# Full-height filter and value products, small loads on a second queue, and four reorderings, in a two-block sequence kernel

## The chip, the cores and the metric

The kernel runs on one core of a Trainium2 chip. The metric is the device time of one launch in microseconds (us): 2917.35 is the median of three runs (2915.61 to 2918.12). The engines that matter are TensorE (PE; its weight loads are listed apart as PEld), VectorE (DVE), ScalarE (ACT), GpSimd (POOL) and SyncE (SP), which issues nearly all transfers.

## The reference

The input is x (512 tokens of 1024 numbers) and a context ctx (256 tokens). Two blocks follow one another, all in float32.

- First block: `mod = silu(c) @ w_ada + b_ada` gives shifts, scales and gates ("vectors"). `rms_norm(x)` and `rms_norm(ctx)` are modulated with them and projected with `w_in` into keys, values, queries and gates of retention and mLSTM scans, whose outputs are merged; then a SwiGLU layer and a final `rms_norm`.
- Second block: four layers; before each, `cond @ w_mod[layer] + b_mod[layer]` gives its vectors.
  - Layers 0 and 3: latent attention, softmax over 768 keys.
  - Layer 1: windowed attention with a sink, `p = softmax(concat(scores + [sink]))`, `out = p @ v`.
  - Layer 2: Hyena, two long convolutions with filters `h = (sin(...) @ f_w3) * exp(-t * deltas)`.
  - Each layer ends with `x = x + gate * rmsnorm(y @ w_out, g_post)`; the last x is the output.

## The kernel before

Activations lie transposed in SBUF: eight tiles (k) of 128 features by 512 tokens (256 for ctx). A product in float32 accuracy is three float32r products on a high and a low part (`mac`, L441 to L443: hi*hi, hi*lo, lo*hi). `split` (L397, L398) makes the parts, the high one on ACT and the low one on DVE. Weights come through four `raw` buffers of 512 KB, issued on SP (`wload`, L403).

The kernel is written as generators that `weave` runs side by side in given proportions. A scheduler then orders each engine's instructions; every engine executes its own in order, and so does SP's queue.

- Start (`first_block`): SP issues small vectors and the filters' small tables, then x, ctx and the weights `w_ada` (L504 multiplies them, two transfers a step, four steps a vector). x and ctx are transposed (L490), squared and summed (L231, L235), normed (`apply`: L570 and L576 on DVE, L575 on ACT, for eight tiles of x and then eight of ctx). The first pair's keys are one complete product for each of two heads; rope (L781 to L783) follows, then the keys of ctx.
- Filters (`filter_unit`, L1873, L1874), woven into the SwiGLU layer: `ps = x @ w + x[0:64] @ l`, where x holds 64 high rows over 64 low rows, w the high weights twice, l the low weights in 64 rows. There are 48 such pairs.
- Windowed attention: `stageA` makes scores and softmax of a block of 128 queries for four heads one after the other, `stageB` transposes the probabilities and multiplies with the values, stored as 64 high columns beside 64 low ones: `v` (128 columns) by p.hi (L1739), `v.hi` (64 columns) by p.lo (L1738, L1741). `softmax` closes each head by itself: a sink exponential (L1387), a sum (L1388), a reciprocal (L1389).
- Hyena: four channel groups c; group c's convolutions (i = 0 for x, 1 for ctx) are woven with the projections of c+1. After the third round come ctx's convolution of the last group and nine steps of x's, woven with the next layer's vectors (`bg`, eight steps) and the layer end's first loads (`end`).
- Layer end: groups of 256 tokens: product, copy and squares, root of the mean square (PE, DVE, POOL), its spread over partitions (L1373), scaling and adding x (L1308, L1309), in layer 3 transposes and stores (L1340 to L1342).

Of the kernel before, what the change touches and what calls it, by code (L numbers as in the profile page):

```python
# [254 lines left out]
class Kern:  # L255
# [347 lines left out]
    def first_block(self):  # L603
# [35 lines left out]
        def norm1():  # L639
            self.need(1)  # L640
            G1 = c1.tile([128, 2, 8], F32, name="G1")
# [5 lines left out]
            X.clear()  # L647
            yield from self.apply(C, rms[1].rstd(), NC, G1[:, 1, :], mv[0][:, 1, :], hc, KT)
            C.clear()

        todo = [(0, 0), (0, 1), (1, 0), (1, 1)]
        units = chain(setup, self.filters(todo[:FS], 1), late)
        weave((chain(inputs[0], sums(rms[0], X)), 17), (islice(units, U0), U0), self.mods(MA))
        self.log_sigmoid(lg, lgt, 8)
        mods = chain(self.mods(M0 - MA)[0], root(rms[0]), self.mods(8 - M0)[0])
        weave((chain(inputs[1], sums(rms[1], C)), 17), (islice(units, U1), UW * U1), (mods, 9 - MA))
        rms[1].root()
        W = I["w_in"][0]
        ahead = [self.wv(W, 512)]
        weave((norm1(), 16), (islice(units, UB), UB))  # L660
        cf = {}
        for k, (o, n) in self.coff["first"].items():
            if n == 512:
                cf[k] = self.b()
                nc.sync.dma_start(cf[k], I["k_first"][:, o:o + n])
# [132 lines left out]
        def dense(pair, ml):  # L798
# [5 lines left out]
            o.K = [self.bhl() for _ in range(2)]  # L804
            for u in range(2):
                ps = self.proj(wk, hx, N, 128 * u)
# [230 lines left out]
        weave((dense(0, False), ND), (chain(idle(GD), gates()), 10 + GD), (units, UC))  # L1037
# [206 lines left out]
    def layer_end(self, l, W, tail):  # L1244
# [19 lines left out]
        def product(z):  # L1264
# [4 lines left out]
            act = [x[:, s] for x in acts.pop(z) + [self.kept.pop((i, t0))] for s in (slice(0, 256), slice(256, 512))]  # L1269
            o.y = [self.b() for _ in range(KT // 2)]  # L1270
            o.rs = Rms(self, 256, D)
# [58 lines left out]
        self.pending = rest(len(groups) - 1)  # L1330
        self.h, self.ws = h, {}

# [43 lines left out]
    def softmax(self, S, P, rd, scale, sink=None):  # L1376

        nc = self.nc
        s = self.sp.tile([128, 8], F32, tag="sm", name="sm")
        nc.vector.tensor_reduce(s[:, 0:1], S, AX.X, ALU.max)  # L1380
        if sink is None:
            nc.vector.tensor_scalar(s[:, 1:2], s[:, 0:1], -scale, None, ALU.mult)  # L1382
        else:
            nc.vector.tensor_scalar(s[:, 1:2], s[:, 0:1], -scale, sink[1], ALU.mult, ALU.min)
        nc.scalar.activation(P, S, AF.Exp, bias=s[:, 1:2], scale=scale, accum_out=s[:, 2:3])  # L1385
        if sink is not None:
            nc.scalar.activation(s[:, 3:4], sink[0], AF.Exp, bias=s[:, 1:2])  # L1387
            nc.vector.tensor_tensor(s[:, 2:3], s[:, 2:3], s[:, 3:4], ALU.add)  # L1388
        nc.vector.reciprocal(rd, s[:, 2:3])  # L1389
# [48 lines left out]
    def mla(self, j, ctx_out, bg, end):  # L1438
# [131 lines left out]
        def stageA(h, i):  # L1570
# [3 lines left out]
            o["P", i], o["rd", i] = [], self.sp.tile([128, 4], F32, tag="rd", name="rd")  # L1574
            for qt in range(n // 128):
# [10 lines left out]
                self.softmax(ps[:, off:off + tot], P, o["rd", i][:, qt:qt + 1], scale)  # L1586
                o["P", i].append(P)
                yield
# [40 lines left out]
    def swa(self, bg, end):  # L1629
# [73 lines left out]
        def stageA(g, i, qt):  # L1703
# [4 lines left out]
            rd = self.sp.tile([128, 4], F32, tag="rd", name="rd")  # L1708
            for v in range(4):
# [11 lines left out]
                h = 4 * g + v  # L1721
                self.softmax(ps[:, 512 - nb:768], P, rd[:, v:v + 1], scale, (self.sink[:, h:h + 1], nsink[:, h:h + 1]))
                Ps.append(P)
                yield
            U[g, i, qt] = (Ps, rd, list(range(k0, k1)) + [4, 5], sl)

        def stageB(g, i, qt):
# [3 lines left out]
            for z in range(nb + LS):  # L1731
                if z < nb:
                    pt.append(self.transposed([P[:, 128 * z:128 * z + 128] for P in Ps]))
                if z >= LS:
                    v, p = V[blocks[z - LS]], pt.pop(0)
                    last = z == nb + LS - 1
                    if last:
                        nc.tensor.matmul(out[:64, :], v[:, g, 0], p.lo, start=False, stop=False)  # L1738
                    nc.tensor.matmul(out, v[:, g], p.hi, start=z == LS, stop=last)  # L1739
                    if not last:  # L1740
                        nc.tensor.matmul(out[:64, :], v[:, g, 0], p.lo, start=False, stop=False)  # L1741
# [34 lines left out]
    def filter_setup(self):  # L1776
# [5 lines left out]
        nc.sync.dma_start(w1, I["c_f_w1_2"][0])  # L1782
        zs = []
        for n, kz in ((N, "k_fz"), (NC, "k_fzc")):
            z = self.t(n)[0:33, :]
            nc.sync.dma_start(z, I[kz])
            zs.append(z)
        for i, nm in enumerate(("c_f_b1_2", "c_f_b2_2", "c_f_freq_2")):
            nc.sync.dma_start(sm[:, i:i + 1], I[nm].rearrange("a (f o) -> (a f) o", o=1))
# [316 lines left out]
```

## Time and profile before

| | |
|---|---|
| median of three runs | 2917.35 us (2915.61 to 2918.12) |
| profiled execution | 2918.76 us, its span 2917.0 us |
| granted TensorE clock, mean | 0.982 of full speed |
| PE, DVE, ACT, POOL busy | 2787.1, 1814.9, 1334.4, 128.8 us |
| HBM read and written | 273.90 and 42.21 MB |

"Busy" of PE counts modelled ends, so the distance between the starts of two neighbouring products is the better measure of what one takes. Idle time of another engine matters only where PE waits for it. 1.76 us of the execution lie outside the span.

### The profile page before, as it was taken

Reading aid. Unit: us, or ns where it says so; the run is one execution under the profiler, and the core shown is the slowest. Engines: PE = TensorE matmul, PEld = TensorE weight load, DVE = VectorE, ACT = ScalarE, POOL = GpSimd, SP = SyncE. Lnnn points to the kernel's source line nnn. Section 1 sums busy time; section 2 is a strip of 40 time slices with the busy share of each in tenths; the row PEclk is TensorE's granted clock in tenths of the full one; section 3 lists DMA queues with packets and bytes.
Section 4 is the critical chain, followed back from the end, with each engine's and each line's share of the span. In section 5 each row is a group of like instructions: output and inputs, shape, how many; then the busy total and the mean of one; then the engine's idle time right before and its main releaser. Section 6 shows DMA issues by size and latency. Waiting matters only on the chain. (4 is left out here: it accounts for less than half of the span.)

```text
span 2917.0 us, 44103 instructions
## 1 busy us (share of the span) xinstructions
PE 2787.1 (96%) x17106; PEld 2364.2 (81%) x17106; DVE 1814.9 (62%) x3775; ACT 1334.4 (46%) x2610; POOL 128.8 (4%) x158
## 2 busy tenths in 40 slices
PE   7999999999999999999999999989999998999998
PEld 4888878887777787888889877778888886887887
DVE  6665455555655556246768577788576777754774
ACT  4344344346455433345555566675332223544553
POOL 1000000000000000000000000000021122000000
PEclk8999999999999999999999999999999999999998
DMA  7233232544555536321234241123132226432122
GB/s 264 86 111 123 73 101 84 168 154 141 164 158 163 170 112 209 108 67 44 68 93 156 64 131 42 35 71 117 62 95 84 84 80 195 130 97 63 56 82 69
DMA packets 365830, 318.98 MB, mean 109 GB/s; under 512 B 17511, under 2 KB 326517, under 8 KB 365620
## 3 DMA queue, kind: packets, MB, share of 16 engines
q1 hardware_dynamic: 365204, 315.99, 35.2%
q8 instruction: 134, 2.20, 0.3%
q14 instruction: 76, 0.62, 0.1%
q0 software_dynamic: 416, 0.17, 0.0%
HBM read 273.90 MB, written 42.21 MB: 108 GB/s over the span
## 5 line engine op out<-in xcount | busy, mean ns | idle before, releaser
L441 PE MATMUL mm<-b,whi 128*128 128x512 f32 (+1 forms) x2548 | 895.8, 352 | 4.7 <-ACT whi L397 2.5
L443 PE MATMUL mm<-b,wlo 128*128 128x512 f32 (+1 forms) x2548 | 887.3, 348 | 1.2 <-DVE wlo L398 1.1
L442 PE MATMUL mm<-b,whi 128*128 128x512 f32 (+1 forms) x2548 | 887.6, 348 | 0.0
L441 PEld LDWEIGHTS mm<-b,whi 128*128 128x128 f32 x2548 | 486.1, 191 | 74.4 <-issue 5.8
L443 PEld LDWEIGHTS mm<-b,wlo 128*128 128x128 f32 x2548 | 486.1, 191 | 62.0 <-DVE wlo L398 2.3
L442 PEld LDWEIGHTS mm<-b,whi 128*128 128x128 f32 x2548 | 486.5, 191 | 60.2 <-issue 0.8
L398 DVE TENSOR_TENSOR wlo<-raw,whi 128x1024 fp32r<-128x1024 f32 (+3 forms) x286 | 292.0, 1023 | 239.7 <-ACT whi L397 224.1
L397 ACT CAST whi<-raw 128x1024 fp32r<-128x1024 f32 (+3 forms) x286 | 252.3, 885 | 397.1 <-PE mm L442 253.9
L443 PE MATMUL mm<-b 128*128 128x256 f32 (+1 forms) x628 | 189.4, 302 | 0.5 <-DVE b L398 0.3
L1385 ACT ACTIVATE P<-mm,sm 128x768 f32<-128x768 f32 (+3 forms) x176 | 127.9, 727 | 116.6 <-DVE sm L1382 68.4
L441 PE MATMUL mm<-b 128*128 128x256 f32 (+1 forms) x500 | 158.2, 318 | 8.4 <-ACT P L1385 4.6
L441 PE MATMUL mm<-b,P 128*128 128x256 f32 x560 | 161.8, 289 | 4.0 <-ACT b L575 2.8
L442 PE MATMUL mm<-b,P 128*128 128x256 f32 x560 | 160.4, 286 | 0.9 <-DVE b L576 0.8
L442 PE MATMUL mm<-b 128*128 128x256 f32 (+1 forms) x500 | 153.0, 307 | 0.4 <-DVE b L398 0.3
L1380 DVE TENSOR_REDUCE sm<-mm 128x1 f32<-128x768 f32 (+3 forms) x176 | 128.6, 733 | 39.7 <-PE mm L1583 23.8
L245 POOL TENSOR_TENSOR rs<-rs,mhalf 128x2 f32<-128x2 f32 (+1 forms) x44 | 42.3, 962 | 2427.2 <-DVE rs L244 2279.8
L398 DVE TENSOR_TENSOR t<-mm,t 128x512 fp32r<-128x512 f32 (+1 forms) x208 | 136.5, 663 | 15.3 <-ACT t L397 14.1
L397 ACT CAST t<-mm 128x512 fp32r<-128x512 f32 (+1 forms) x208 | 116.0, 569 | 54.8 <-PE mm L1395 51.6
L235 DVE TENSOR_TENSOR t<-t 128x256 f32<-128x256 f32 (+1 forms) x216 | 92.5, 441 | 71.9 <-ACT t L231 69.4
L1395 PE MATMUL mm<-ct,P 128*128 128x128 f32 x768 | 122.8, 276 | 13.0 <-ACT P L1385 8.2
L231 ACT ACTIVATE t<-b 128x256 f32<-128x256 f32 (+1 forms) x252 | 100.7, 431 | 67.7 <-DVE b L1101 40.9
L443 PEld LDWEIGHTS mm<-b 128*128 128x128 f32 x628 | 120.6, 192 | 5.6 <-DVE b L398 1.3
(351 smaller groups left out, 5129.7 us busy)
## 6 DMA issues: line engine op xcount, KB each, us to landing
raw<-in_w_mod_dram SPq DMA_DIRECT2D x96, 512.0 KB, 4.4
raw<-in_w_ada_dram SPq DMA_DIRECT2D x48, 512.0 KB, 3.9
raw<-in_w_in_dram SPq DMA_DIRECT2D x48, 512.0 KB, 4.0
raw<-in_w_ffn_in_dram SPq DMA_DIRECT2D x44, 512.0 KB, 4.1
raw<-in_c_w_in_dram SPq DMA_DIRECT2D x32, 512.0 KB, 4.3
raw<-in_a_w_in_dram SPq DMA_DIRECT2D x28, 512.0 KB, 4.1
ks<-t SPq DMA_DIRECT2D x48, 256.0 KB, 2.8
raw<-ks SPq DMA_DIRECT2D x24, 512.0 KB, 3.3
```

The lines of the kernel that those rows point to most:

```text
L231: self.k.nc.scalar.activation(sq, x, AF.Square)
L235: self.k.nc.vector.tensor_tensor(self.acc, self.acc, sq, ALU.add)
L245: nc.gpsimd.tensor_tensor(s[:, 4:4 + nt], s[:, :nt], self.k.mhalf[:, :nt], ALU.pow)
L397: self.nc.scalar.copy(dst.hi, src)
L398: self.nc.vector.tensor_tensor(dst.lo, src, dst.hi.bitcast(F32), ALU.subtract)
L441: nc.tensor.matmul(ps, l.hi, r.hi, start=start and i == 0, stop=False)
L442: nc.tensor.matmul(ps, l.hi, r.lo, start=False, stop=False)
L443: nc.tensor.matmul(ps, l.lo, r.hi, start=False, stop=stop and i == n - 1)
L1380: nc.vector.tensor_reduce(s[:, 0:1], S, AX.X, ALU.max)
L1385: nc.scalar.activation(P, S, AF.Exp, bias=s[:, 1:2], scale=scale, accum_out=s[:, 2:3])
L1395: self.nc.tensor.transpose(ps[:, 128 * i:128 * i + 128], b, self.ident)
```

## The change

Seven edits:

1. Filters: l gets 64 zero rows (set by POOL), and the second product takes all 128 rows of x.
2. Values of the windowed attention: the low-probability product takes all 128 columns of v, always after the high one.
3. Start: x's loads come first on SP; the small vectors and tables are issued on ACT's queue; ctx's loads come after the keys' weights. Four of the vectors' steps run beside x's transposes.
4. First keys: two banks gather both heads' products tile by tile as x is normed. Then come rope, woven with the whole of ctx's transposes, sums, root and norm (`norm1c`).
5. Softmax: one sink exponential, one sum and one reciprocal for four heads (or four query tiles).
6. End: the last group's products are scaled from PSUM, transposed into token-major banks at once, and multiplied by the root at the end, where x (transposed earlier) is added; half of the stores go on ACT's queue.
7. Vectors among convolutions: layer 3's eight vector steps move from the last Hyena stage into its three rounds (3, 3, 2).

```
-        first = self.rows(False, nc.sync)
+        inputs = [self.load_T(I["x"][0], N, X), self.load_T(I["ctx"][0], NC, C)]
+        next(inputs[0])
+        first = self.rows(False, nc.scalar)
         next(first)
-        setup = self.filter_setup()
+        setup = self.filter_setup(nc.scalar)
         next(setup)
-        inputs = [self.load_T(I["x"][0], N, X), self.load_T(I["ctx"][0], NC, C)]
-        for g in inputs:
-            next(g)
...
+        weave((chain(inputs[0], sums(rms[0], X)), 17), (islice(units, U0), U0), self.mods(M0 - 3))
+        self.log_sigmoid(lg, lgt, 8)
+        mods = chain(self.mods(3)[0], root(rms[0]), self.mods(8 - M0)[0])
+        weave((islice(units, U1), UW * U1), (mods, 12 - M0))
+        W = I["w_in"][0]
+        ahead = [self.wv(W, 512)]
+        next(inputs[1])
+        def norm1c():
+            yield from inputs[1]
+            yield from sums(rms[1], C)
+            rms[1].root()
+            yield
...
             yield from self.apply(C, rms[1].rstd(), NC, G1[:, 1, :], mv[0][:, 1, :], hc, KT)
...
+                banks = [self.mm() for _ in range(2)]
+                for k, _ in enumerate(norm1()):
+                    for u in range(2):
+                        self.mac(banks[u], [(wk[k][:, 128 * u:128 * u + 128], hx[k])], k == 0, k == KT - 1)
+                    yield
...
-        weave((dense(0, False), ND), (chain(idle(GD), gates()), 10 + GD), (units, UC))
+        start = dense(0, False)
+        weave((islice(start, KT), KT))
+        cf.update(tables())
+        weave((islice(start, 2), 2), (norm1c(), 25))
+        weave((start, ND - 2), (chain(idle(GD), gates()), 10 + GD), (units, UC))
...
+    def last(self, proj, t0, rs, G):
...
+        for k in range(KT):
+            ps = proj(k)
+            y = self.t(256)
+            nc.vector.tensor_scalar(y, ps, G[:, k:k + 1], None, ALU.mult)
+            rs.add(ps)
+            ys.append((k, y))
+            if len(ys) > 1:
+                turn(*ys.pop(0))
...
+        rs.root()
+        for h in range(2):
+            for j in range(2):
+                o = xt[j, h]
+                nc.vector.scalar_tensor_tensor(o, T[j][:, 512 * h:512 * h + 512], rs.cols[j], o, ALU.mult, ALU.add)
+                (nc.scalar if j else nc.sync).dma_start(self.out[t0 + 128 * j:t0 + 128 * j + 128, 512 * h:512 * h + 512], o)
...
+        def end(rd):
+            if sink is not None:
+                nc.vector.tensor_tensor(top[:, 0:n], sink, top[:, 4:4 + n], ALU.add)
+                nc.scalar.activation(top[:, 0:n], top[:, 0:n], AF.Exp)
+                nc.vector.tensor_tensor(sums[:, 0:n], sums[:, 0:n], top[:, 0:n], ALU.add)
+            nc.vector.reciprocal(rd[:, 0:n], sums[:, 0:n])
...
+                    nc.tensor.matmul(out, v[:, g], p.hi, start=z == LS, stop=False)
+                    nc.tensor.matmul(out, v[:, g], p.lo, start=False, stop=z == nb + LS - 1)
...
-            ws.append((w, l[0:64, :]))
+            nc.gpsimd.memset(l[64:128, :].bitcast(F32), 0.0)
+            ws.append((w, l))
...
-                        nc.tensor.matmul(ps, x[0:64, :], l, start=False, stop=True)
+                        nc.tensor.matmul(ps, x, l, start=False, stop=True)
...
-            weave((cv, HC), (dense(c + 1), 16))
+            weave((cv, HC), (dense(c + 1), 16), (islice(bg[0], 3 - c // 2), 3 - c // 2))
         cv = conv(0, 3)
-        weave((conv(1, 3), 14), (islice(cv, HT), HT), bg, (end, 3 + 3 * AP))
+        weave((conv(1, 3), 14), (islice(cv, HT), HT), (end, 3 + 3 * AP))
```

The scheduler's order shows three places. First SP's queue at the start of the kernel before, from the end of the small loads (`fw`, `ftc` are filter tables; `b` holds x and ctx, `raw` weights, `xd` a copy of x):

```order
L1791 DMA fw_155<-in_c_f_w_2_dram 64x64
L1793 DMA ftc<-in_k_ftime_dram 128x6
L484 DMA b<-in_x_dram 128x512 x8
L484 DMA b<-in_ctx_dram 128x512 x4
L403 DMA raw<-in_w_ada_dram 128x1024 x16
L403 DMA raw<-in_w_in_dram 128x4x256 x2
L403 DMA raw<-in_w_ada_dram 128x1024 x2
L645 DMA xd<-b 128x512 x8
```

and SP's queue from its first transfer on, after the change:

```order
L293 DMA ct<-in_k_parts_dram 128x388
L484 DMA b<-in_x_dram 128x512 x8
L403 DMA raw<-in_w_ada_dram 128x1024 x16
L403 DMA raw<-in_w_in_dram 128x4x256 x2
L484 DMA b<-in_ctx_dram 128x512 x4
L403 DMA raw<-in_w_ada_dram 128x1024 x2
L644 DMA xd<-b 128x512 x8
```

Fifteen small loads have left the queue ahead of x, and ctx has moved behind the keys' weights, but stays ahead of the last two transfers of `w_ada`.

Second, DVE at the first keys, before (128x512 is x, 128x256 ctx; `wlo` weights; L781 begins rope):

```order
L576 SCALAR_TENSOR_TENSOR b<-t,mv_191,b 128x512
L576 SCALAR_TENSOR_TENSOR b<-t,mv_191,b 128x256 x2
L570 SCALAR_TENSOR_TENSOR t<-b,G_614,mm 128x256 x3
L576 SCALAR_TENSOR_TENSOR b<-t,mv_191,b 128x256 x3
L570 SCALAR_TENSOR_TENSOR t<-b,G_614,mm 128x256 x3
L576 SCALAR_TENSOR_TENSOR b<-t,mv_191,b 128x256
L398 TENSOR_TENSOR wlo<-raw,whi 128x1024
L576 SCALAR_TENSOR_TENSOR b<-t,mv_191,b 128x256 x2
L781 SCALAR_TENSOR_TENSOR t<-mm,b 128x512
```

and DVE there after the change (L791 to L793 are rope, L491 ctx's copies out of PSUM, L235 its sums, L244 its root; the first head's rope stands just ahead):

```order
L491 COPY b<-mm 128x256
L235 TENSOR_TENSOR t<-t 128x256 x3
L791 SCALAR_TENSOR_TENSOR t<-mm,b 128x512
L792 SCALAR_TENSOR_TENSOR t<-t,b 128x512
L235 TENSOR_TENSOR t<-t 128x256
L793 TENSOR_TENSOR t<-t 128x512
L235 TENSOR_TENSOR t<-t 128x256 x2
L398 TENSOR_TENSOR b<-t,b 128x512
L244 TENSOR_SCALAR rs<-mm 128x2
L570 SCALAR_TENSOR_TENSOR t<-b,G_571,mm 128x256 x3
```

Before, ctx was copied and summed long before, and its norm stood ahead of rope; now its copies, sums, root and norm stand behind the norm of x and among both heads' rope.

Third, PE in the last convolution stage, before (L504 are the vectors, L1973 transposes, `<-t,b` and `<-P,b` 128x512 the convolutions' products):

```order
L441 MATMUL mm_24579<-P,b 128x512
L504 MATMUL mm<-raw,condc_221 32x256 x4
L442 MATMUL mm_24579<-P,b 128x512
L443 MATMUL mm_24579<-P,b 128x512
L1973 MATMUL mm_24592<-ct,t 128x128 x4
L441 MATMUL mm_24617<-t,b 128x512
L504 MATMUL mm<-raw,condc_221 32x256 x4
L442 MATMUL mm_24617<-t,b 128x512
```

and PE there after the change (`mm<-b` 128x256 is the layer end's product, L2051 the transposes):

```order
L442 MATMUL mm_24332<-P,b 128x512
L443 MATMUL mm_24332<-P,b 128x512
L441 MATMUL mm<-b 128x256
L442 MATMUL mm<-b 128x256
L2051 MATMUL mm_24345<-ct,t 128x128
L443 MATMUL mm<-b 128x256
L441 MATMUL mm<-b 128x256
L2051 MATMUL mm_24345<-ct,t 128x128 x3
L442 MATMUL mm<-b 128x256
```

The vectors' products are gone from between the convolutions, and from the second convolution on the layer end's products stand there.

## Rows read from the trace of the kernel before

**Rows 1.** The page, part 1: busy time of each engine, share of the span, instructions.

```profile
PE 2787.1 (96%) x17106; PEld 2364.2 (81%) x17106; DVE 1814.9 (62%) x3775; ACT 1334.4 (46%) x2610; POOL 128.8 (4%) x158
```

**Rows 2.** Stretches by engine: us, busy time (instructions), granted clock, DMA share, GB/s.

```profile
650.00:1008.00 358.00, 358.00 (x1633) 269.55 (x1632) 202.72 (x298) 190.53 (x257) 0.00 (x0) 1.00 0.51 160
1660.00:2000.00 340.00, 308.41 (x1983) 259.45 (x1982) 267.00 (x728) 217.40 (x540) 0.80 (x1) 0.97 0.25 75
2100.00:2400.00 300.00, 299.42 (x1812) 265.80 (x1810) 207.53 (x365) 87.75 (x146) 60.25 (x72) 1.00 0.27 82
```

**Rows 3.** Timeline of PE in a filter: start us, us, line, product, rows*columns of the weights.

```profile
653.52 0.40 PE L1873 MATMUL mm<-b 128*128 128x512 f32 x1
653.85 0.50 PE L1874 MATMUL mm<-b 64*128 64x512 f32 x1
654.28 0.50 PE L1873 MATMUL mm<-b 128*128 128x512 f32 x1
...
656.34 0.40 PE L442 MATMUL mm<-b,whi 128*128 128x512 f32 x1
```

**Rows 4.** The 64-row filter product's line: count, shortest/median/longest ns, first and last start.

```profile
L1874 PE MATMUL mm<-b x48: 497/500/507, 653.8 to 1004.4; 64*128 64x512 f32 x48
```

**Rows 5.** Timeline of PE among the windowed attention's value products.

```profile
1696.68 0.66 PE L1395 MATMUL mm<-ct,P 128*128 128x128 f32 x4
1697.09 0.47 PE L1741 MATMUL mm<-t,b 128*64 128x512 f32 x1
...
1697.63 0.39 PE L1741 MATMUL mm<-t,b 128*64 128x512 f32 x1
1697.86 0.40 PE L443 MATMUL mm<-b,wlo 128*128 128x512 f32 x1
```

**Rows 6.** Timeline of SP's queue at the start: first issue, us of issuing, count.

```profile
1.18 0.36 SPq L339 DMA_DIRECT2D rows<-in_c_dram  x1
...
8.24 3.75 SPq L484 DMA_DIRECT2D b<-in_x_dram  x8
```

**Rows 7.** Timeline of PE at the start: first keys of x, first keys of ctx.

```profile
56.73 0.77 PE L441 MATMUL mm<-b,whi 128*128 128x512 f32 x1
...
69.97 0.28 PE L441 MATMUL mm<-whi,b 128*128 128x256 f32 x1
```

**Rows 8.** Groups of DVE, 40 to 84 us: shapes, count, busy us, mean ns, idle before.

```profile
L570 DVE SCALAR_TENSOR_TENSOR t<-b,G,mm 128x512 f32<-128x512 f32 x8 | 5.8, 742 | 0.9 <-PE mm L1373 0.9
...
L570 DVE SCALAR_TENSOR_TENSOR t<-b,G,mm 128x256 f32<-128x256 f32 x8 | 3.5, 471 | 0.0
...
L235 DVE TENSOR_TENSOR t<-t 128x256 f32<-128x256 f32 x7 | 2.9, 416 | 0.2
```

**Rows 9.** The softmax's sink exponential, who waited for it, and its reciprocal.

```profile
L1387 ACT ACTIVATE sm<-sink,sm x96: 280/283/316, 1654.1 to 1979.0; 128x1 f32<-128x1 f32 x96
...
  DVE sm L1388: 16.5, 22
...
L1389 DVE RECIPROCAL rd<-sm x176: 143/162/166, 1305.2 to 2842.3; 128x1 f32<-128x1 f32 x176
```

**Rows 10.** Last convolution stage: the vectors' products alone (L504), then all, by stretch.

```profile
2411.00:2435.50 24.50, 7.28 (x80) 1.89 (x80) 0.93 0.72 237
2435.50:2450.10 14.60, 3.03 (x32) 0.67 (x32) 0.79 0.86 276
...
2435.50:2450.10 14.60, 8.63 (x56) 5.08 (x55) 10.32 (x17) 3.06 (x5) 6.52 (x8) 0.79 0.86 276
```

**Rows 11.** Timeline of the end: last product, the roots spread, last copy.

```profile
2900.75 0.28 PE L443 MATMUL mm<-b 128*128 128x256 f32 x1
...
2904.10 0.43 PE L1373 MATMUL mm<-ct,rs 128*128 128x128 f32 x2 [1.10 <-POOL rs L245]
...
2912.34 0.58 ACT L1341 COPY b<-mm 128x512 f32<-128x512 f32 x1 [3.31 <-PE mm L1340]
```

**Rows 12.** The page, part 6: a weight transfer of the vectors, KB, us to landing.

```profile
raw<-in_w_mod_dram SPq DMA_DIRECT2D x96, 512.0 KB, 4.4
```

More of the change, by code (lines that the diff above doesn't have):

```diff
@@ L647, in norm1, with tables @@
             X.clear()
+        todo = [(0, 0), (0, 1), (1, 0), (1, 1)]
+        units = chain(setup, self.filters(todo[:FS], 1), late)
+        weave((chain(inputs[0], sums(rms[0], X)), 17), (islice(units, U0), U0), self.mods(M0 - 3))
[10 more added lines that the diff above has]
+            yield
+            G1 = have["G1"]
             yield from self.apply(C, rms[1].rstd(), NC, G1[:, 1, :], mv[0][:, 1, :], hc, KT)
             C.clear()
[L651 to L660, printed above, removed]
-        cf = {}
[L662 to L665, printed above, removed]
+        have = {}
+        cf = {}
+        def tables():
+            for k, (o, n) in self.coff["first"].items():
+                if n == 512:
+                    t = self.b()
+                    nc.sync.dma_start(t, I["k_first"][:, o:o + n])
+                    yield k, t
         RH = self.bhl()
@@ L804, in dense @@
             o.K = [self.bhl() for _ in range(2)]
+            banks = []
+            if out == {(pair, ml): o}:
+                banks = [self.mm() for _ in range(2)]
[3 more added lines that the diff above has]
+                    yield
             for u in range(2):
[L806 removed]
+                ps = banks[u] if banks else self.proj(wk, hx, N, 128 * u)
                 if ml:
@@ L1269, in product @@
             act = [x[:, s] for x in acts.pop(z) + [self.kept.pop((i, t0))] for s in (slice(0, 256), slice(256, 512))]
+            o.rs = Rms(self, 256, D)
+            if l == 3 and z == len(groups) - 1:
+                yield from self.last(lambda k: self.proj(ws[k], act, 256), t0, o.rs, m[2][:, 0, :])
+                return
             o.y = [self.b() for _ in range(KT // 2)]
-            o.rs = Rms(self, 256, D)
             for k in (5, 6, 7, 3, 4, 0, 1, 2) if z == len(groups) - 1 else (0, 1, 2, 5, 6, 7, 3, 4) if z else range(KT):
@@ L1374, in over_columns, with softmax, step @@
         return ps[:m, :128 * len(cols)]
-    def softmax(self, S, P, rd, scale, sink=None):
+    def softmax(self, n, scale, sink=None, nsink=None):
         nc = self.nc
[L1379 to L1389, printed above, removed]
+        top, sums = (self.sp.tile([128, 8], F32, tag=x, name=x) for x in ("sm", "sums"))
+        def step(j, S, P):
+            b = top[:, 4 + j:5 + j]
+            nc.vector.tensor_reduce(top[:, j:j + 1], S, AX.X, ALU.max)
+            if sink is None:
+                nc.vector.tensor_scalar(b, top[:, j:j + 1], -scale, None, ALU.mult)
+            else:
+                nc.vector.tensor_scalar(b, top[:, j:j + 1], -scale, nsink[:, j:j + 1], ALU.mult, ALU.min)
+            nc.scalar.activation(P, S, AF.Exp, bias=b, scale=scale, accum_out=sums[:, j:j + 1])
+        def end(rd):
[4 more added lines that the diff above has]
+            nc.vector.reciprocal(rd[:, 0:n], sums[:, 0:n])
+        return step, end
     def transposed(self, blocks):
@@ L1574, in stageA @@
             o["P", i], o["rd", i] = [], self.sp.tile([128, 4], F32, tag="rd", name="rd")
+            step, end = self.softmax(n // 128, scale)
             for qt in range(n // 128):
@@ L1585, in stageA @@
                 P = self.P(tot)
-                self.softmax(ps[:, off:off + tot], P, o["rd", i][:, qt:qt + 1], scale)
+                step(qt, ps[:, off:off + tot], P)
                 o["P", i].append(P)
+                if qt == n // 128 - 1:
+                    end(o["rd", i])
                 yield
@@ L1708, in stageA @@
             rd = self.sp.tile([128, 4], F32, tag="rd", name="rd")
+            step, end = self.softmax(4, scale, self.sink[:, 4 * g:4 * g + 4], nsink[:, 4 * g:4 * g + 4])
             for v in range(4):
@@ L1720, in stageA @@
                 P = self.P(nb + 256)
-                h = 4 * g + v
-                self.softmax(ps[:, 512 - nb:768], P, rd[:, v:v + 1], scale, (self.sink[:, h:h + 1], nsink[:, h:h + 1]))
+                step(v, ps[:, 512 - nb:768], P)
                 Ps.append(P)
+                if v == 3:
+                    end(rd)
                 yield
```

46 lines of the change are left out of this document (31 added, 15 removed).

## The prediction

> **What bounds the kernel now.** I read the page's busy shares first: PE is busy 2787 of 2917 us, the next engine 62% [rows 1]. So a part is worth what it takes out of PE's own stream, or out of the 130 us in which PE waits. Then the busy time by stretch, to see which of the two holds where. During the filters (650 to 1008 us) PE is busy 358.00 of 358 us, in the first Hyena rounds 299.4 of 300, and in the windowed attention only 308.4 of 340, with DVE at 267 [rows 2]. In the first two, work added to or taken from PE moves the end one for one; in the third a chain through DVE and ACT holds PE for 31.6 us. Then the timelines of the four places that the change rewrites: start, filters, last convolution stage, end. The reader is to look there at the distance between the starts of neighbours, not at the printed durations, since the ends are modelled.
>
> **Filters (edit 1).** A full 512-column product follows its neighbour after 0.23 us [rows 5]. Around the 64-row products it takes longer: from 653.52 to 656.34 us run three pairs and one product, seven in 2.82 us [rows 3], where seven at 0.23 us are 1.61. So 1.21 us are lost on three pairs, 0.40 on each; the loss falls on the 64-row product and equally on the 128-row one behind it. There are 48 pairs [rows 4]: 19.4 us. With both products over 128 rows I take the whole of it as gone, for PE has no idle time there that could take its place, while DVE (203 us) and ACT (191) are far from full [rows 2]. Bounds: nothing, if the loss has another cause, and 19.4. The zero rows are set by POOL, which is idle in this stage (0.00 us, [rows 2]); without that cover each of the four filters would start late by two such fills.
>
> **Values (edit 2).** 88 low products (L1738, L1741; 22 key blocks in each of four head groups) go from 64 columns of weights to 128. Their successor starts 0.23 us after them already [rows 5], so I take 0. The high part of the last block now goes first, but the low part closes the sum later by as much: also 0.
>
> The Trainium skill (TensorEngine Tiling (Array Packing), section Tiling Modes) says that changing the tiling mode drains the engine, and lists 128x64 as a mode of its own. By that rule these 88 products cost what the filters' do, 88 times 0.40 or 35 us, and the change would give them back. For 64 rows the trace fits the rule; for 64 columns it does not, since the step to a 128-column product took 0.23 us [rows 5].
>
> **Softmax (edit 5).** In the windowed attention 96 heads close one by one; after the change 24 groups of four do. 72 sink exponentials of 0.283 us leave ACT (20 us), 72 reciprocals of 0.162 us and as many sums, which I price alike, leave DVE (23 us), and three quarters of DVE's 16.5 us of waiting for the exponential go as well (12 us) [rows 9]. So DVE gets 35 us. What PE gets lies between 0 (the products are held by scores, maximum, exponential and bank, which stay) and the 31.6 us it now waits. I take 12, a third of DVE's relief, since the exponential and the split of the probabilities remain in the chain. In the latent attention 80 reciprocals become 24, 9 us of DVE; PE is nearly full there, so I take 1, between 0 and 9. Together 13.
>
> **Vectors among convolutions (edit 7).** In the last stage (2411 to 2450 us) the vectors' products fill PE for 7.28 and 3.03 us, at a mean granted clock of about 0.88; in the second half PE is busy only 8.63 of 14.6 us and the DMA engines 0.86 [rows 10]. At full clock these 10.3 us are 9.1, and in the convolution rounds, where PE is full [rows 2], all of that is added. In the stage they leave, the first 24.5 us lose 7.3, but these products also covered waits of the convolutions' chain; I take 5 as gained, nearer to the 7.3 than to nothing. The second 14.6 us shrink to the 5.6 us of other work, about 5 at full clock, as the layer end's products now stand in the gaps: a gain of 9.6. So 14.6 less 9.1: 5.5 us gained. Bounds: 1.2 (only the products' own 10.3 go) and 8.4 (the first stretch gains its whole 7.3 and the second ends at 4.4).
>
> **End (edit 6).** The last product ends at 2901.03, the span at 2917.0 [rows 11]: 16.0 us. What stays is the way to the root's spread, 3.1 us (2901.03 to 2904.10), then four scalings of 512 columns at 0.74 [rows 8], 3.0, and the last store, from the copy's end at 2912.92 to 2917.0, 4.1: 10.2 us. That saves 5.8. Ahead of it PE gets 32 more transposes, at 0.41 us for four [rows 5], 3.3 us. Net gain 2.5, between 6 (transposes in gaps) and a loss of 3 (products that wait for PSUM banks behind DVE's burst of the group before).
>
> **Start (edits 3 and 4).** x's loads go from 8.24 us on SP's queue to 1.18 [rows 6], 7.1 us earlier. ctx's loads leave their place but still stand ahead of the last two `w_ada` transfers, whose products precede the first keys on PE; so I move these only by the 7.1: from 56.73 [rows 7] to 49.7. From there DVE decides. It still has 13 of x's 16 norm instructions (0.72 us each by their busy time, 9.4), then, by the order shown, ctx's four copies (priced as its sums, 1.7) and sums (2.9), both ropes with their splits (eight instructions like x's, at 0.7, 5.6), the root (about 2.5 without the copy that the end has) and ctx's first tile (2.3) [rows 8, 11]: 24.4 us. So the first keys of ctx start at 74.1, where they now start at 69.97 [rows 7]: a loss of 4. What is late is no longer the weights but ctx's norm, which used to be done while they came. Bounds: a gain of 8 if ctx's work fits into gaps of x's, and a loss of 10 if rope's tables, now behind three more weight transfers on SP, arrive late by about 6. The fifteen issues on ACT I price at nothing, since they run beside x's transfers; without that cover the first products wait for some of the same 7 us, as they do now.
>
> **Sum.** -19.4 - 13 - 5.5 - 2.5 + 4 = -36.4. Against the profiled execution's 2918.76 that is 2882.4; the median of the runs shown is 1.4 lower, so 2881.
>
> **Rivals.**
> 1. The filters' loss is not one of 64 rows (but, say, of the operands' banks): 19.4 less, 2900. For it: the cause is only inferred. Against: the neighbours on both sides lose, and only there. 0.08.
> 2. Every change of the array's shape drains: 35 us more, 2846. Against it the 0.23 us. 0.05.
> 3. The windowed attention stays as it is, because the banks' cycle through maximum and exponential holds it: 12 less, 2893. For it: those two remain unchanged. Against: DVE is the busiest helper there and is relieved of 35 us. 0.14.
> 4. The start gains its 8 us in place of losing 4: 2869. For it: ctx's copies and sums depend on nothing but its loads. Against: the order puts them behind x's norm on DVE. 0.12.
> 5. Slower: the vectors' 16 weight transfers share four `raw` buffers with the weights and filters of the convolution rounds. If each holds back the next weights by its own landing, 4.4 us [rows 12], PE loses 70 us there: 2951. It decides the sign from 2.6 us a transfer on (36.4 and 5.8 over 16). Against: the DMA engines are busy 0.27 there [rows 2]. 0.03.
> 6. Some part does not do what it says, in a way that none of these names: 0.03.
>
> **How the numbers follow.** 0.55 for the forecast, with its own range of 2867 to 2896. The range of 2858 to 2904 takes in the bounds of start, softmax and convolutions, rivals 1, 3 and 4, and leaves out 2, 5 and what lies at the ends of several bounds at once. A measurement of this kernel tells 0.2% (5.8 us) from no change. Faster holds in all cases but the fifth and a part of the sixth: 0.94; same 0.02; slower 0.04.
>
> **What would show it.** Filters: starts 0.23 us apart around the two lines, and that stage 19 us shorter. Values: unchanged distances. Windowed attention: PE's idle time near 20 us. Last convolution stage: about 25 us up to the work that now ends at 2450, and the three rounds 9 longer. Start: first keys of x near 50 us, of ctx near 74, PE idle between them. End: 10 us from the last product to the end of the span. Most wrong would be the forecast if the filters' distances stayed at 0.43, or if the attention gave nothing or all of its 31.6 us.

## The result and the profile after

The changed kernel takes 2931.51 us (median of four, 2928.45 to 2934.07) beside 2916.48 for the kernel before on the same chip: ratio 1.0052, 95% interval 1.0035 to 1.007. It is slower by 15 us; 2881 was forecast, and 2904 was the upper end.

A table by stage finds the 47 us between forecast and trace. A shift is worked out so: of products found in both traces by line and shape, the k-th start after less the k-th before, and the median over a short stretch. The table gives what each stage adds to the shift.

| stage | forecast | after | shift behind it |
|---|---|---|---|
| start (to 150 us) | +4 | +24.7 | 24.7 |
| first block up to the filters | 0 | +2.1 | 26.8 |
| filters | -19.4 | -16.0 | 10.8 |
| latent attention, layer 0 | -1 (with layer 3) | -1.6 | 9.2 |
| windowed attention | -12 | -2.3 | 6.9 |
| three convolution rounds (from 6.7) | +9.1 | +8.3 | 15.0 |
| last convolution stage | -14.6 | -4.1 | 10.9 |
| PE up to the last product (from 10.6) | +3.3 | +6.5 | 17.1 |
| behind the last product | -5.8 | -6.5 | 10.6 |

From one execution to the next a stage that isn't changed moves by up to 4.5 us, so the small differences of the table are read over several runs below.

Part 1 of the profile's page for the kernel after (busy, share, instructions) answers to [rows 1]:

```profile
PE 2769.6 (95%) x17120; PEld 2370.9 (81%) x17120; DVE 1798.5 (61%) x3593; ACT 1321.4 (45%) x2533; POOL 130.4 (4%) x166
```

PE is busy 17.5 us less in a span that is 10.6 longer: what was saved in products came back as waits. The same work as in [rows 2], by stretch (us, then PE, PEld, DVE, ACT, POOL, clock, DMA):

```profile
676.00:1020.00 344.00, 341.62 (x1634) 270.63 (x1633) 201.69 (x298) 191.09 (x258) 3.12 (x6) 1.00 0.54 167
1669.00:2007.00 338.00, 306.62 (x1985) 260.69 (x1984) 258.15 (x611) 204.57 (x471) 0.70 (x1) 0.98 0.25 75
2107.00:2415.00 308.00, 307.52 (x1925) 268.49 (x1923) 211.50 (x378) 89.18 (x146) 57.85 (x72) 1.00 0.34 104
```

The filters are shorter and still full. In the windowed attention PE's idle time is what it was, 31.4 us for 31.6, though DVE and ACT have less to do: 8.9 and 12.8 us of busy time less than in [rows 2]. In a filter (timeline of PE; answers to [rows 3]) the starts now stand 0.23 us apart on both lines:

```profile
680.29 0.39 PE L1951 MATMUL mm<-b 128*128 128x512 f32 x1
680.53 0.39 PE L1952 MATMUL mm<-b 128*128 128x512 f32 x1
...
681.69 0.39 PE L441 MATMUL mm<-b,whi 128*128 128x512 f32 x1
```

The start is where it was lost. Timeline of PE after (in brackets the idle time ahead and its releaser; answers to [rows 7]):

```profile
44.27 0.69 PE L513 MATMUL mm<-ct,acc 128*128 128x128 f32 x2 [0.54 <-DVE acc L509]
52.26 1.08 PE L504 MATMUL mm<-raw,condc 128*32 128x256 f32 x8 [7.30 <-DMA raw<-in_w_ada_dram]
53.27 0.69 PE L1440 MATMUL mm<-ct,rs 128*128 128x128 f32 x2
...
57.19 1.22 PE L441 MATMUL mm<-b,whi 128*128 128x512 f32 x2 [1.59 <-ACT b L575]
...
72.40 0.44 PE L490 MATMUL mm<-ct,b 128*128 128x128 f32 x2 [1.36 <-DVE t L791]
...
82.91 1.01 PE L242 MATMUL mm<-mean,t 128*128 128x1 f32 x4 [5.40 <-DVE t L235]
84.96 0.69 PE L1440 MATMUL mm<-ct,rs 128*128 128x128 f32 x2 [1.03 <-POOL rs L245]
86.76 0.58 PE L441 MATMUL mm<-whi,b 128*128 128x256 f32 x1 [1.11 <-ACT b L575]
```

Three things stand there. The vector that the norm needs is ready at 44.3 (L513), but the roots' spread (L1440) stands on PE behind a product that no key needs, the ninth vector step, whose transfer is last on SP's queue; so the keys of x come at 57.19, where they came at 56.73. In the kernel before the same vector was ready 5.3 us later, but the ninth step's first product stood 0.5 us earlier:

```profile
49.57 0.69 PE L513 MATMUL mm<-ct,acc 128*128 128x128 f32 x2 [0.54 <-DVE acc L509]
51.79 1.08 PE L504 MATMUL mm<-raw,condc 128*32 128x256 f32 x8 [1.53 <-DMA raw<-in_w_ada_dram]
```

Then ctx is transposed, squared, summed and rooted while PE has nothing else: its keys start 16.8 us later than before. And the clock falls; by stretch, after:

```profile
0.00:10.00 10.00, 0.00 (x0) 0.00 (x0) 3.42 (x21) 0.00 (x0) 7.19 (x18) 1.00 0.63 186
10.00:60.00 50.00, 32.98 (x209) 14.75 (x210) 29.80 (x81) 24.07 (x39) 1.08 (x2) 0.75 0.91 312
70.00:90.00 20.00, 8.82 (x37) 6.76 (x36) 13.77 (x31) 10.23 (x24) 0.70 (x1) 0.64 0.07 17
```

and of the kernel before, two of the same stretches:

```profile
0.00:10.00 10.00, 0.43 (x1) 0.18 (x1) 6.32 (x43) 4.72 (x9) 7.37 (x18) 1.00 0.34 71
10.00:60.00 50.00, 39.13 (x232) 19.45 (x233) 31.17 (x74) 22.03 (x42) 1.74 (x2) 0.74 0.92 319
```

From 10 us on the DMA engines are nine tenths busy in both kernels. Issuing earlier carried 1.15 MB more in the first 10 us, not 7 us of everything behind.

The end, PE after, where the last group of 256 tokens takes over (answers to [rows 11]):

```profile
2884.44 0.28 PE L443 MATMUL mm<-b,wlo 128*128 128x256 f32 x1
2886.09 0.61 PE L242 MATMUL mm<-mean,t 128*128 128x1 f32 x4 [1.37 <-DVE t L235]
2887.79 0.43 PE L1440 MATMUL mm<-ct,rs 128*128 128x128 f32 x2 [1.10 <-POOL rs L245]
2887.98 0.46 PE L441 MATMUL mm<-b 128*128 128x256 f32 x1
2888.23 0.42 PE L442 MATMUL mm<-b 128*128 128x256 f32 x1
```

The root of the group before now stands ahead of the last group's first product. PE waits twice (2.5 us) and then runs products at 0.21 us where 0.12 is usual (16 products, up to 2891.4). From the last product, which ends at 2917.85, to the end of the span are 9.8 us, near the 10.2 forecast.

### The profile page after: what moved, and what is told of

Read it like the earlier page. It is cut to its first block, busy times and chain, and to the rows that moved or that the text cites. A ratio compares the mean times of both kernels' runs of the same rounds, so it can differ in the third digit from the quotient of the medians.

```text
span 2927.6 us, 43848 instructions
## 1 busy us (share of the span) xinstructions
PE 2769.6 (95%) x17120; PEld 2370.9 (81%) x17120; DVE 1798.5 (61%) x3593; ACT 1321.4 (45%) x2533; POOL 130.4 (4%) x166
## 5 line engine op out<-in xcount | busy, mean ns | idle before, releaser
L441 PE MATMUL mm<-b 128*128 128x256 f32 (+1 forms) x500 | 158.6, 320 | 10.6 <-ACT b L397 6.2
L1470 PE MATMUL mm<-ct,P 128*128 128x128 f32 x768 | 122.8, 278 | 10.3 <-ACT P L1456 6.0
L235 DVE TENSOR_TENSOR t<-t 128x256 f32<-128x256 f32 (+1 forms) x216 | 92.7, 441 | 60.3 <-ACT t L231 57.5
```

What stands on the lines that cost most here:

```text
L235: self.k.nc.vector.tensor_tensor(self.acc, self.acc, sq, ALU.add)
L441: nc.tensor.matmul(ps, l.hi, r.hi, start=start and i == 0, stop=False)
L1470: self.nc.tensor.transpose(ps[:, 128 * i:128 * i + 128], b, self.ident)
```

## The experiments

Ratios are to the kernel before on the same chip, with 95% intervals.

**Parts of the change.** Edit 1 alone:

```
-            ws.append((w, l[0:64, :]))
+            nc.gpsimd.memset(l[64:128, :].bitcast(F32), 0.0)
+            ws.append((w, l))
```

> The kernel before with edit 1 alone (filters' second product over 128 rows). Theory: the loss is one of 64-row products, and nothing later takes the gain back: 16 us faster (what the filter stage of the changed kernel gave), ratio 0.9945. My forecast's figure was 19.4 us, ratio 0.9933. Rival (the loss has another cause, and the stage got shorter because of the late start, with weights already there): under 6 us, ratio above 0.998.

Measured: 0.9949 (0.9936 to 0.9963); the stage gives 16.3 us by its shift, and the span ends 15.7 earlier. The theory holds; over all traces with this edit the stage gives 14.8 to 17.5.

Edits 3 and 4 undone (`first_block`, `filter_setup` and the first weave as before):

> The changed kernel with edits 3 and 4 (start) undone. Theory: the start alone costs 24.7 us, so this is 10 us faster than the kernel before: ratio 0.9965. Rival (the late start was in part paid back later, since weights and DVE had a lead in the stages behind it): the gain of undoing is 10 us or less, ratio 1.001 or more.

Measured: 0.9953 (0.994 to 0.9965), span 9.3 us under before. The theory holds: the start costs some 25 us (20 by the two profiled executions, 29 by the two ratios), and nothing later pays it back.

Edit 7 undone:

```
-            weave((cv, HC), (dense(c + 1), 16), (islice(bg[0], 3 - c // 2), 3 - c // 2))
+            weave((cv, HC), (dense(c + 1), 16))
```

> The changed kernel with edit 7 (vectors among convolutions) undone. Theory: the vectors' products stood in the last stage as cover of a chain through DVE and ACT that stays; the move adds 8.3 us to the rounds and takes 4.1 from the last stage, so undoing it gives 4 us: ratio to the kernel before 1.0037 where the changed kernel has 1.0052. My forecast: undoing it costs 5.5 us, ratio 1.007.

Measured: 1.0023 (1.0012 to 1.0033), below both figures and on the theory's side of 1.0052. With edit 7 the rounds lose 8.3 to 8.5 us in six traces and the last stage gives 1.3 to 4.2; without it the rounds lose nothing. So edit 7 costs 4 to 7 us.

Edits 1, 2, 5 and 6 alone:

> Edits 1, 2, 5 and 6 alone (3, 4 and 7 undone). Theory: the stages add up, 16 us from the filters, 2 from the softmax, none from the end: 2916.5 - 18 = 2898, ratio 0.994. Rival (interaction): more than 5 us away from the sum of what the two kernels beside it show.

Measured: 0.9937 (0.9923 to 0.995), 2901.72 us. The stages add up.

**The 64-row products.** The kernel before, with pairs in twos:

```
+                    for x, ps in zip(xs, banks):
+                        nc.tensor.matmul(ps, x, w, start=True, stop=False)
+                    for x, ps in zip(xs, banks):
+                        nc.tensor.matmul(ps, x[0:64, :], l, start=False, stop=True)
```

> The kernel before with the filters' 48 pairs in twos: two 128-row products, then two 64-row ones. Theory (each change of the row count costs 0.2 us, so a pair loses 0.40): half of the changes go, the filter stage is 24 x 0.40 = 9.6 us shorter, and inside a group starts stand 0.23 apart. Rival (each 64-row product itself is slow): 0.40 a product stays, no change.

Measured (one run): the stage is 8.3 us shorter, half of what edit 1 gives. Timeline of PE there:

```profile
654.46 0.63 PE L1874 MATMUL mm<-b 128*128 128x512 f32 x2
655.02 0.74 PE L1876 MATMUL mm<-b 64*128 64x512 f32 x2
655.69 0.74 PE L1874 MATMUL mm<-b 128*128 128x512 f32 x2
656.36 0.73 PE L1876 MATMUL mm<-b 64*128 64x512 f32 x2
657.14 0.50 PE L441 MATMUL mm<-b,whi 128*128 128x512 f32 x1
```

Eight products take 2.68 us where eight at 0.23 are 1.84: 0.84 over four changes, 0.2 each. It is the change of the row count that costs, not the product. One detail was expected otherwise: inside a group the starts do not stand 0.23 apart. The step across a change takes 0.33 us and the one behind it 0.34 to 0.35, for 128 rows as for 64, so each change is paid in two steps.

**The start.** ctx's work back among the vectors (keys still tile by tile):

```
-        weave((islice(units, U1), UW * U1), (mods, 12 - M0))
+        weave((chain(inputs[1], sums(rms[1], C)), 17), (islice(units, U1), UW * U1), (mods, 12 - M0))
+        rms[1].root()
```

> The changed kernel with ctx's loads right behind x's and ctx's transposes, copies, sums and root back among the vectors, where the kernel before has them; loads first, small loads on ACT's queue and the first keys tile by tile stay. Theory: the 24.7 us of the start are ctx's work, which used to lie in the time in which PE waits for w_ada's transfers and now stands behind the first keys, where PE waits for it (70.6 to 86.8 us) at a clock that falls to half. So ctx's keys come near 70 us, the start loses under 5 us, and the whole is 20 us faster than the changed kernel: ratio to the kernel before 0.998. Rival 1 (the order of loads costs it): the first keys of x move to 60 us or later and half or more of the loss stays. Rival 2 (the tile-by-tile keys cost it, as two banks are held and DVE paces them): the loss stays at 20 us or more.

Measured: 1.0015 (1.0003 to 1.0026); the start loses 15.6 us in place of 24.7. ctx's keys come at 73.49, 13 us sooner, but most of the loss now lies behind them. The theory fell: ctx's place is only part of it. Next, ctx's norm ahead of rope as well:

```
-        weave((islice(start, 2), 2), (norm1c(), 9))
-        weave((start, ND - 2), (chain(idle(GD), gates()), 10 + GD), (units, UC))
+        weave((norm1c(), 9))
+        weave((start, ND - KT), (chain(idle(GD), gates()), 10 + GD), (units, UC))
```

> As the changed kernel with ctx's work back among the vectors, and besides ctx's norm complete ahead of rope on DVE, as in the kernel before, with the rest of the first projections woven with the gates again. Loads first and tile-by-tile keys stay. Theory (order on DVE and the gates' cover): of the 15 us that were left at least 11 go; work behind the gates stands within 4 us of its time in the kernel before, and the whole is 11 to 15 us faster than with ctx early alone, ratio near 0.997. Rival (two banks held by the tile-by-tile keys, or the order of the loads): 8 us or more of the 15 stay, ratio 1.0 or more.

Measured: 1.0029 (1.002 to 1.0038), start 20.0 us late. The share `ND - KT` (the proportion in which `weave` takes the projections against the gates) was my mistake: the gates' products went ahead of ctx's keys, which came only at 98.66, and PE waited among them:

```profile
97.52 1.49 PE L714 MATMUL mm<-ct,P 128*64 128x128 f32 x6 [6.22 <-DVE P L704]
```

With edit 7 undone and the end mended (the step less that **The end** below shows) it had the same fault (0.999, 0.998 to 0.9999; start 22.3 late):

> The same, with edit 7 undone and the last group's first product ahead of the root. Theory: the stages add up to what edits 1, 2, 5, 6 with the repaired end gave, as tile-by-tile keys gain nothing where DVE paces the norm: 2896 to 2900 us, ratio 0.992 to 0.994. Rival (tile-by-tile keys gain up to 5 us once ctx is out of the way): ratio under 0.9915.

With the kernel's own share, `(start, ND)`:

> The changed kernel with ctx's work back among the vectors, ctx's norm complete ahead of rope on DVE, and the first projections and gates in the order on PE of the kernel before (that kernel's shares). Loads first and tile-by-tile keys stay. Theory (where ctx's work and rope stand on DVE, and what covers the gates, is the whole loss): the work behind the start stands within 4 us of its time in the kernel before, and the whole is 20 us or more faster than the changed kernel: ratio 0.997 to 0.999. Rival (the tile-by-tile keys or the order of loads cost it): 8 us or more of the 24.7 stay.

Measured: 0.9966 (0.9953 to 0.9979). Behind the start PE stands 0.7 us from its time before; ctx's keys start at 72.6, and then PE runs without a wait:

```profile
72.63 0.35 PE L441 MATMUL mm<-whi,b 128*128 128x256 f32 x1 [1.15 <-DVE pc L346]
73.06 0.28 PE L441 MATMUL mm<-whi,b 128*128 128x256 f32 x1
```

The theory holds: the loss is ctx's work behind the first keys, rope ahead of its norm, and gates that have too little work to cover them. How the last 15 us divide between rope's place and the gates' share is not shown, since this run changes both. The early loads and the tile-by-tile keys together neither cost nor gain. With edit 7 undone and the end mended:

> The same, with edit 7 undone and the last group's first product ahead of the root. Theory: the stages add up to what edits 1, 2, 5, 6 with the repaired end gave: 2893 to 2900 us, ratio 0.992 to 0.994. Rival (tile-by-tile keys and loads first gain up to 5 us once ctx is out of the way): ratio under 0.9915.

Measured: 2900.58 us, 0.9943 (0.993 to 0.9957), just above the theory's 2900 us and 0.994; the rival's 0.9915 is out.

Why did the first keys not come 7 us earlier? The changed kernel with the ninth step behind ctx's keys:

```
             self.have.add(i)
+            if i == 1:
+                yield
```

> The changed kernel with the ninth vector step (two transfers, 16 products) behind ctx's keys. Theory (PE's order ate the gain): the roots' spread comes at 45 to 46 us in place of 53.3, the first keys at 48 to 51 in place of 57.2, ctx's keys 6 to 8 us sooner than 86.8, and the loss of the start falls from 24.7 to 16 to 18 us. Rival (bytes): the keys' weights or x's norm come no sooner, the first keys stay at 55 or later.

Measured (one run): the first keys of x at 46.65, those of ctx at 79.18:

```profile
43.62 0.60 PE L1442 MATMUL mm<-ct,rs 128*128 128x128 f32 x4
46.65 1.22 PE L441 MATMUL mm<-b,whi 128*128 128x512 f32 x2 [2.44 <-ACT b L577]
```

PE's order ate the gain: with it, the keys of x come 10.5 us sooner. The start still loses 19.5, a little more than expected; ctx's chain stays. In the kernels with the old start the same edit gave nothing:

> The kernel with start and vectors undone, and the ninth step of the vectors (two transfers of 512 KB, 16 products, which the first keys don't need) moved behind the first keys. Theory: PE's order holds the first keys back; the roots' spread stands behind products that wait for these transfers, until 55.0 us, while the second vector is ready at 49.6. The first keys come 3 to 5 us earlier (52 to 54 us in place of 56.7) and the whole ends 3 us earlier. Rival: weights on SP's queue set the pace up to 80 us, with the DMA engines at 0.8 to 0.97; then later products wait instead, and the end moves by less than 1 us.

Measured: 0.9932 (0.9906 to 0.9958), first keys at 56.29 for 56.41; no gain, as the rival had it for the end. The first key's wait there (2.47 us) ends with a small copy on DVE (L346), which stands behind the splits of both halves of the keys' weights; ACT's part of the second split comes only at 53.5 (49.6 without the edit). With x first besides:

> As the one with the ninth step later, and x's and ctx's loads first on SP with the small loads on ACT's queue; ctx's work stays where it was in the kernel before. Theory: the transfers ahead of the keys are bound by the DMA engines (0.81 to 0.97 busy from 10 to 60 us in both kernels), so starting 7 us earlier gives only what the engines carry more in the first 10 us (186 for 71 GB/s, 1.15 MB, 3.7 us at 310 GB/s): first keys 3 to 4 us earlier still. My forecast's way of reckoning: the whole 7.1 us. Rival: the vectors' products on PE and their four buffers hold the transfers: under 1 us.

Measured: 0.9949 (0.9934 to 0.9964), first keys at 59.24, 3 us later, which no theory had. SP's queue (timeline) shows why:

```profile
14.34 1.97 SPq L403 DMA_DIRECT2D raw<-in_w_ada_dram  x4
16.43 7.10 SPq L647 DMA_DIRECT2D xd<-b  x7
25.82 1.19 SPq L403 DMA_DIRECT2D raw<-in_w_ada_dram  x2
```

The stores of x had moved ahead of twelve `w_ada` transfers: 2.1 MB at 319 GB/s are 6.6 us, less 3.7 gained. That fits the bytes, but was seen afterwards. With ninth step and stores behind the keys' weights:

> The kernel whose last group starts ahead of the root, with the ninth vector step and the eight stores of x (2 MB) behind the weights of the keys. Theory: up to the first keys the DMA engines are the bound, so bytes that are taken away ahead of them count: the second transfer of keys' weights lands 3 us sooner than with the ninth step moved alone, and the first keys come at 53 us in place of 56.3. Rival: DVE paces this part (norms of x and ctx, 19 us, then rope), so the keys of ctx come no sooner and the end moves by less than 1 us.

Measured: 0.9931 (0.9915 to 0.9948), first keys at 57.09: no gain, and the rival holds. With the stores out of the way the second split comes at 54.3 on ACT, straight behind the norm's first tile, and the first key waits for the same copy, so it is the order on DVE and ACT that holds it.

**The windowed attention.** No maximum (all but the first lines as in edit 5):

```
+            if sink is None:
+                nc.vector.tensor_reduce(top[:, j:j + 1], S, AX.X, ALU.max)
```

> The kernel whose last group starts ahead of the root, with the windowed attention's 96 maxima and shifts left out (the exponential is taken of the scores divided by 64, less the sink, so its probabilities are others). DVE loses about 80 us there. Theory 1: PE is held by scores, maximum, exponential and the bank's release; without the maximum PE's idle time in that stage falls from 31 us to under 18. Theory 2: it is held behind the probabilities, by transposes, split and their products (ACT's exponential and copy, DVE's low part); PE's idle time stays above 25 us.

Measured (one run): the stage is 28.2 us shorter than in the kernel before. The same work by stretch, without maximum:

```profile
1651.00:1962.00 311.00, 297.79 (x1975) 257.17 (x1974) 192.72 (x435) 197.82 (x465) 0.69 (x1) 0.99 0.27 81
```

and in the kernel that it was made from:

```profile
1645.00:1987.00 342.00, 310.53 (x1979) 263.65 (x1978) 257.62 (x609) 203.90 (x469) 0.69 (x1) 0.97 0.24 74
```

PE's idle time falls from 31.5 to 13.2 us: theory 1. The run also takes 65 us of work from DVE (257.62 to 192.72), so it does not tell the maximum's place in the chain from DVE's relief. What stands between a maximum and its exponential is seen on DVE in the kernel after:

```profile
1752.33 0.42 DVE L1451 TENSOR_REDUCE sm<-mm 128x1 f32<-128x256 f32 x1
1752.98 0.69 DVE L1423 TENSOR_TENSOR t<-mm,b 128x512 f32<-128x512 f32 x1 [0.22 <-ACT t L1415]
...
1757.18 0.20 DVE L1455 TENSOR_SCALAR sm<-sm,nsink 128x1 f32<-128x1 f32 x1
```

This shift (L1455) starts 4.85 us after its maximum, behind rope and splits of other heads. That is near the worst: the median over the 96 heads is 1.20 us. So the shift alone was moved:

```
-                nc.vector.tensor_scalar(b, top[:, j:j + 1], -scale, nsink[:, j:j + 1], ALU.mult, ALU.min)
+                nc.gpsimd.tensor_scalar(b, top[:, j:j + 1], -scale, nsink[:, j:j + 1], ALU.mult, ALU.min)
```

> The kernel whose last group starts ahead of the root, with the 96 shifts of the windowed attention (scale the maximum, lower bound of the sink; one column of 128 numbers) on POOL, which is idle there. On DVE a shift takes 0.2 us but can stand behind rope of the next keys, 4.85 us in one place of the changed kernel. Theory 1 (the queue in front of the shift holds PE): PE's idle time there falls from 31 us by 4 to 10, and the whole is 3 to 8 us faster. Theory 2 (the maximum's own time, 0.4 to 0.7 us for each of 96 heads and behind rope itself, holds PE): no change within 2 us. Rival: POOL's longer instruction (0.7 us for a like one) lengthens each chain: up to 10 us slower.

Measured: 2890.68 us, 0.9911 (0.9897 to 0.9925): the fastest of all, though its interval overlaps that of the kernel it was made from. PE's idle time there is 29.2 us (335.00 less 305.77), 2.3 less, between the theories. In the kernels that leave this stage's maxima, shifts and vectors alone it is 30.7 to 31.7 us, so the 2.3 are clear of that; the rest of the 7 us by which the stretch is shorter is busy time of PE, which goes with the granted clock (0.99 for 0.97) from trace to trace. So the queue in front of the shift is a small part of the 18 us. Whether the rest is the maximum's own time or DVE's other load was not split further.

Vectors into those gaps:

> The kernel whose last group starts ahead of the root, with layer 3's eight vector steps moved into the windowed attention, four steps in each of its four groups. Theory: PE has 31 us of gaps there, so most of the 10 us of products cost nothing; the last convolution stage gives 4 us as it did in the changed kernel: 0 to 5 us faster than without the move. Rival: PE's gaps there are chain latency in which a vector step of 16 products stands in the way; the stage grows by 8 us or more, and the whole is 4 us slower.

Measured: 0.9947 (0.9929 to 0.9964) for 0.9927 without the move; the stage grows by 6.2 us over the kernel before, the last convolution stage gives 3.0. The intervals overlap, so slower is not shown, but there is no gain: PE's idle time falls only to 29.3 us. The rival holds in its sign.

**The end.** One step less ahead of the last group's first product:

```
             xs.append(t)
-        yield
         T = [self.mm2() for _ in range(2)]
```

> Edits 1, 2, 5, 6 as in the kernel with start and vectors undone, but the last group's loads no longer take a step of their own, so that its first product stands ahead of the root of the group before on PE. Theory: of the 6.5 us that PE loses in edit 6, about 4 come from that order (1.37 and 1.10 us of waits, and 16 products at 0.21 us where 0.12 is usual, under a clock that fell during the waits), so the last product ends 4 us sooner, and the whole is 4 us faster than that kernel. Rival: the 32 transposes and their banks cost it all; no change.

Measured: 0.9927 (0.9909 to 0.9945), 2896.55 us. PE loses 3.05 us up to the last product; in all seven traces with this mend it is 3.1, and 5.3 to 6.5 in the ten without. The ratio without it was 0.9937, with an overlapping interval; the gain is read from the traces. The roots' spread waits 0.65 us there:

```profile
2861.31 0.50 PE L242 MATMUL mm<-mean,t 128*128 128x1 f32 x4
...
2862.91 0.32 PE L1417 MATMUL mm<-ct,rs 128*128 128x128 f32 x1 [0.65 <-POOL rs L245]
```

## Why the prediction was wrong

- **Start (+4, was +24.7): the step that failed most.** "I move these only by the 7.1" took loads that are issued earlier for transfers that all land as much earlier. The norm's vector was ready 5.3 us earlier (44.27 for 49.57), but the ninth step, now close behind ctx's loads, was not (52.26 for 51.79). Nor did it follow PE's order from that last transfer to the roots' spread; the first keys came at 57.2, not 49.7. (Sixteen small loads left SP's queue, not fifteen; nothing hangs on it.) The 24.4 us of DVE work from x's keys to ctx's were 29.6. And the count ended at ctx's keys: behind them another 8 us go, in products at the lower clock (0.21 for 0.12 us) and in a gates' chain that PE now reaches with less work in between.
- **Last convolution stage (-14.6, was -4.1).** "The second 14.6 us shrink to the 5.6 us of other work" held PE for the bound. It was the convolutions' chain through ACT, DVE and POOL: PE idles 10.3 of 36.0 us there, where it idled 10.1 of 39.1 us with the vectors between. The waits of PE after (2426 to 2462 us, the stretch of [rows 10]; us in all, times, longest):

```profile
PE mm L442 <- DVE b L398: 2.6, 2, 1.4
PE mm L441 <- DVE t L2097: 1.6, 1, 1.6
PE mm L441 <- DVE P L398: 1.5, 1, 1.5
PE mm L2051 <- DVE t L2042: 1.4, 2, 1.1
PE mm L2092 <- POOL P L2074: 1.2, 2, 0.9
```

- **Windowed attention (-12, was -2.3).** Rival 3, at 0.14, was right. I took a third of DVE's relief, 35 us. The relief itself was mis-sized: DVE's busy time fell by 8.9 us, not 23, since a sum or reciprocal printed at 0.15 us often has its follower 0.07 us behind it, and the addition of the sink that each group now needs was left out. More than that, sums, sink exponentials and reciprocals come behind the exponential. Without what stands ahead of it, maximum and shift, PE idles 18 us less, of which the shift's queue is 2.3; in the rest DVE's lighter load has an unknown part. In this edit's traces the stage moves by -3.2 to +2.4 us, without it by -0.3 and +1.1: no gain can be told. The Trainium skill (VectorE: DVE Perf Modes, section Rules for kernel authors) calls `tensor_reduce` on the hot path DVE's slowest operation and advises restructuring. The 28 us without it agree with the advice; slowest it is not here, as 512 columns take 0.68 us, like the `tensor_tensor` of a split.
- **Filters (-19.4, was -16.0).** Right in kind; the 0.40 us of the pairs that I read was the upper bound, 0.34 the mean over 48.
- **End (-2.5, was 0).** The transposes (3.1 measured with the mend, 3.3 forecast) and the tail (9.8 for 10.2) were right. The bare step that changes the order at the group's border cost the other 3.4.
- **Rounds (+9.1, was +8.3)** were right, and rival 5's transfers did not hold them (PE 307.52 busy of 308).
- **Values (0)** were right: the step from L1818 to the next product is 0.22 us with 128 columns, as it was with 64 (0.24 in the median of 88, before and after), so no 35 us came back as the Trainium skill's rule on modes (TensorEngine Tiling (Array Packing), section Tiling Modes) would have had it; for rows the grouped filters agree with it.

```profile
1701.93 0.39 PE L1818 MATMUL mm<-t,b 128*128 128x512 f32 x1
1702.15 0.39 PE L441 MATMUL mm<-b,whi 128*128 128x512 f32 x1
```

The range failed because the start's bounds (-8 to +10) were those of loads and norm alone; the rest of the chain was not in it. And edit 7 as a whole came out at a loss of 4.2 us (4.1 gained, 8.3 paid), below its lower bound of 1.2 gained, which had left out that waits take the products' place.

## What to carry to other kernels

Work that ran while PE waited for transfers cost nothing here, and "out of the way" put it on the path: before moving such work, name what the engine will do in its new place. Where the transfer engines are nine tenths busy, count the bytes ahead of a transfer instead of moving it by its issue; then look at which instruction on the waiting engine stands behind the last transfer. Price a batched softmax by what stands ahead of the exponential, not by what is saved behind it.

## What was not expected

- Each change between 128 and 64 rows of these 512-column products costs 0.2 us, in either direction, and one between 128 and 64 columns nothing that shows.
- After 16 us in which PE was busy under 5 (71.0 to 86.8), products of 256 columns stand 0.21 us apart for 5.6 us, then 0.12: the engine's two levels, 1.2 and 2.4 GHz (granted clock 0.64 in the mean of 70 to 90 us).
- A shift of one column on POOL takes 0.29 us in the median (0.41 in the mean), against 0.20 on DVE.
